# The stationary weights of the down blocks lie at 16 places within 256 bytes, 16 bytes apart, one place per block

## The chip, the core and the metric

The kernel runs on one core of a Trainium2 chip. The metric is the device time of one execution in microseconds. It was run three times, 2055.77, 2059.43 and 2058.96 us, so the median is 2058.96 us.

## What is computed

One transformer block on 256 tokens of width 2048, in float32: an attention and recurrence mixer, and then a layer that picks for every token and each of 8 heads 16 of 16384 experts. The part that matters here is that last layer. Every expert is one row of `down` and one row of `up`:

```python
def chunk(args):
    x_c, e_c, g_c = args
    act = jax.nn.gelu(jnp.einsum('td,thkd->thk', x_c, down[e_c]).astype(jnp.float32),
                      approximate=False) * g_c
    return jnp.einsum('thk,thkd->td', act.astype(up.dtype), up[e_c])
```

`e_c` are the experts picked and `g_c` their softmax weights. The picks come from a product of the token with `wq` (query), compared with keys.

## The kernel before

The kernel doesn't gather rows. It multiplies all 256 tokens by all 16384 rows of `down`, applies gelu, multiplies by a dense table of weights that is zero where an expert was not picked, and multiplies by all of `up`. The 16384 experts are cut into 32 down blocks (d0 to d31) of 512 experts. The 4 query blocks (wq0 to wq3) go through the same code.

A float32 product is made of three matmuls of rounded float32 values: every operand is split into a high part (`wh`, `xH`) and the rest (`wl`, `xL`), and hi*hi, hi*lo and lo*hi are added up in PSUM. `split` (lines 205 to 207) does it for a weight tile: ScalarE writes the high part, VectorE subtracts.

There are two ways to multiply.

- `mm_turn` (lines 365 to 374), for wq and the down blocks: a 128x128 piece of the weights is stationary, and the 256 tokens (`xH`, `xL`) stream by, 256 columns a matmul. One weight tile of 1024 columns makes 24 matmuls, and a block has 8 tiles, so 192 matmuls. Each of them has its own weight load (LDWEIGHTS).
- `mm_sub` (lines 359 to 363), for the mixer and the up blocks: the activations are stationary and the weights stream, 512 columns a matmul.

What sets the place of a weight tile is the list `items`, filled by `add_w` (lines 140 to 143) in the order in which the weights are used; its last field, `shift`, is the number of float32 elements by which the tile is pushed into a buffer that is 64 elements wider than the tile (`WROOM` is 1088). `next_part` (lines 282 to 314) takes the buffer, cuts the slice at `shift` (line 302) and splits into it. There are three buffers for the high and three for the low parts. `XTURN` (line 1049) pushes the streamed activations by 8 elements before the query blocks. `TURN`, 56, is the shift for all query and down blocks.

In the built program the weight buffers and the activations' buffers begin 32 bytes past a multiple of 256, and both the 1088 elements of a buffer (4352 bytes) and the steps between the 128-column pieces (512 bytes) are multiples of 256. "Place" below means the address modulo 256.

The order in time: the mixer up to some 470 us; then wq0 to wq3 and d0 to d13 (`LAG` is 14; lines 1275 to 1293), with the search of the picks and the table of weights (`w_build`, the lookup matmuls of line 1201) run beside them; from some 950 us the up blocks u, four to each of 16 groups, and between them d14 to d31, one down block in front of two up blocks (lines 1295 to 1322).

The gate matmuls of the mixer (`gate_logits`, `mm3`, lines 355 to 357) also have weights as the stationary operand: 16 slices of 24 columns that lie 96 bytes apart in one tile, three matmuls to a slice, with 256 tokens streaming by.

Of the kernel before, what the change touches and what calls it, by code (L numbers as in the profile page):

```python
# [47 lines left out]
TURN, WROOM, XTURN = 56, 1088, 8  # L48
# [19 lines left out]
def kernel(  # L68
# [71 lines left out]
    def add_w(src, n=4096, shift=0):  # L140
        for o in range(0, n, 2048):
            m = min(2048, n - o)
            items.append(("w", src[:, o:o + m], (m + 1023) // 1024, min(m, 1024), shift))
# [20 lines left out]
    nmix = len(items)  # L164
    for j in range(4):
        for h in range(2):
            add_w(wq[j, h], shift=TURN)
    for e in range(LAG):
        for h in range(2):
            add_w(down[e, h], shift=TURN)  # L170
    for g in range(NUG):
        for o in range(2):
            e = 2 * g + 2 + o
            if LAG <= e < NEB:
                for h in range(2):
                    add_w(down[e, h], shift=TURN)
            for q in range(2):
                add_w(up[g, 2 * o + q])
                if 4 <= g < 8:
                    items.append(("ada", 4 * (g - 4) + 2 * o + q))  # L180
# [1237 lines left out]
```

## Time and profile before

| | |
|---|---|
| median of three runs | 2058.96 us |
| the profiled execution | 2058.44 us, of which the span 2056.4 us |
| granted TensorE clock, mean | 0.986 |
| TensorE (PE) busy | 1984.4 us, 97% |
| weight loads (PEld) busy | 1758.6 us, 86% |
| VectorE (DVE) busy | 1451.1 us, 71% |
| ScalarE (ACT) busy | 1017.4 us, 49% |

PE are matmuls and PEld their weight loads, which overlap with them. Matmuls overlap with each other too: one of 256 columns has a duration of about 280 ns, but the next one starts after 113 to 118 ns. The step from one start to the next is therefore read from starts and counts and not from durations. A group in the profile names the line, the engine, the operation, what it writes and reads (buffer numbers left out), the shapes and how often it ran.

### The profile page before, as it was taken

The page shows a single profiled execution, that of the slowest core. Times are in us where ns is not written, and L with a number is a line of the kernel's source. Part 1 is how long each engine was busy: PE and PEld are TensorE (multiplying, and loading weights), DVE is VectorE, ACT ScalarE, POOL GpSimd, SP SyncE. Part 2 cuts the span into 40 slices and gives each one's busy share as a digit, 9 for nine tenths or more (in the row PEclk, how much of TensorE's full clock was granted, in tenths as well). Part 3 has the DMA queues.
Part 4 walks back from the last instruction along what each step waited for, and adds up shares of the span by engine and source line. Part 5 has one row for each costly group of instructions (what it writes and reads, how often), then busy time and mean ns, then how long its engine had stood idle before and what let it go on. Part 6 is the DMA issues. An engine that isn't in the chain of part 4 may idle for free.

```text
span 2056.4 us, 31264 instructions
## 1 busy us (share of the span) xinstructions
PE 1984.4 (97%) x12602; PEld 1758.6 (86%) x12602; DVE 1451.1 (71%) x2149; ACT 1017.4 (49%) x1454; POOL 61.1 (3%) x95
## 2 busy tenths in 40 slices
PE   5999997998999999999999999999999999999998
PEld 4777665788999999999788789889999889999897
DVE  7888999987999666546767766675555555555566
ACT  3545675545447878644444434444444444444442
POOL 0000000000000000001000000000000000000000
PEclk8999998999999999999999999999999999999999
DMA  9898788995555666778767777776565666566563
GB/s 370 334 360 334 267 324 324 348 347 182 177 177 183 241 220 246 257 247 308 256 232 249 282 266 254 255 269 203 198 204 196 212 207 206 204 201 209 198 225 131
DMA packets 75873, 509.12 MB, mean 248 GB/s; under 512 B 8528, under 2 KB 9040, under 8 KB 20176
## 3 DMA queue, kind: packets, MB, share of 16 engines
q1 hardware_dynamic: 63792, 450.50, 60.6%
q0 software_dynamic: 11936, 56.63, 8.2%
q8 instruction: 98, 1.61, 0.3%
q14 instruction: 47, 0.39, 0.1%
HBM read 478.78 MB, written 28.31 MB: 247 GB/s over the span
## 4 chain that ended last, share of the span: by engine, by line
PE 76%; DVE 11%; issue 8%; DMA 3%; ACT 1%; POOL 0%; SPq 0%; DVEq 0%; POOLq 0%; ACTq 0%
PE d L373 11%; PE d L372 11%; PE d L374 10%; PE u L356 8%; PE u L357 8%; PE u L355 8%; DVE wl L207 3%; PE w L1201 3%; DVE av L228 3%; PE wq L373 2%; PE wq L372 2%; PE wq L374 1%; PE y L355 1%; PE y L357 1%; PE y L356 1%
## 5 line engine op out<-in xcount | busy, mean ns | idle before, releaser
L207 DVE TENSOR_TENSOR wl<-raw,wh 128x1024 fp32r<-128x1024 f32 x649 | 789.2, 1221 | 467.0 <-ACT wh L206 464.2
L206 ACT CAST wh<-raw 128x1024 fp32r<-128x1024 f32 x649 | 680.0, 1051 | 813.9 <-PE u L357 374.7
L372 PE MATMUL d<-xH,wh 128*128 128x256 f32 x2048 | 573.2, 280 | 0.0
L373 PE MATMUL d<-xL,wh 128*128 128x256 f32 x2048 | 570.3, 278 | 0.0
L374 PE MATMUL d<-xH,wl 128*128 128x256 f32 x2048 | 569.6, 278 | 0.2 <-DVE wl L207 0.2
L356 PE MATMUL u<-wl,ah 128*128 128x512 f32 x1024 | 399.6, 390 | 3.6 <-DVE wl L207 3.6
L355 PE MATMUL u<-wh,ah 128*128 128x512 f32 x1024 | 398.9, 390 | 0.0
L357 PE MATMUL u<-wh,al 128*128 128x512 f32 x1024 | 398.5, 389 | 0.0
L372 PEld LDWEIGHTS d<-xH,wh 128*128 128x128 f32 x2048 | 385.0, 188 | 0.7
L373 PEld LDWEIGHTS d<-xL,wh 128*128 128x128 f32 x2048 | 384.8, 188 | 0.8
L374 PEld LDWEIGHTS d<-xH,wl 128*128 128x128 f32 x2048 | 384.0, 187 | 0.4 <-DVE wl L207 0.4
L356 PEld LDWEIGHTS u<-wl,ah 128*128 128x128 f32 x1024 | 192.2, 188 | 45.2 <-DVE wl L207 6.0
L357 PEld LDWEIGHTS u<-wh,al 128*128 128x128 f32 x1024 | 192.3, 188 | 40.1
L355 PEld LDWEIGHTS u<-wh,ah 128*128 128x128 f32 x1024 | 192.2, 188 | 39.7
L228 DVE SCALAR_TENSOR_TENSOR av<-av,cb 128x2048 f32<-128x2048 f32 x64 | 145.9, 2285 | 5.5 <-DMA av<-in_ada_w_dram 5.5
L1185 DVE TENSOR_TENSOR oh<-con,idT 128x1024 f32<-128x1024 f32 x64 | 78.0, 1224 | 62.0 <-PE w L1201 62.0
L1206 ACT ACTIVATE oh<-oh,gT 128x128 f32<-128x128 f32 x256 | 83.3, 396 | 25.6 <-DVE oh L1185 25.4
L372 PE MATMUL wq<-xH,wh 128*128 128x256 f32 x256 | 72.7, 285 | 2.5 <-ACT xH L206 2.5
L373 PE MATMUL wq<-xL,wh 128*128 128x256 f32 x256 | 72.6, 284 | 0.0
L374 PE MATMUL wq<-xH,wl 128*128 128x256 f32 x256 | 72.2, 282 | 0.0
L1262 DVE TENSOR_TENSOR acc<-acc,u 128x512 f32<-128x512 f32 x112 | 71.6, 680 | 0.0
L1201 PE MATMUL w<-oh 128*128 128x128 f32 x512 | 69.7, 276 | 0.0
(359 smaller groups left out, 2002.5 us busy)
## 6 DMA issues: line engine op xcount, KB each, us to landing
raw<-in_down_dram SPq DMA_DIRECT2D x128, 1024.0 KB, 5.2
raw<-in_up_dram SPq DMA_DIRECT2D x128, 1024.0 KB, 5.2
av<-in_ada_w_dram SPq DMA_DIRECT2D x64, 1024.0 KB, 7.2
raw<-in_w_a_dram SPq DMA_DIRECT2D x32, 1024.0 KB, 9.3
raw<-in_ada_p_dram SPq DMA_DIRECT2D x16, 1024.0 KB, 6.9
raw<-in_w_out_dram SPq DMA_DIRECT2D x16, 1024.0 KB, 7.9
raw<-in_wq_dram SPq DMA_DIRECT2D x16, 1024.0 KB, 5.2
wd<-stg POOLq DMA_DIRECT2D x8, 2048.0 KB, 7.9
```

What stands on the lines that cost most here:

```text
L206: A.copy(dst_h, src)
L207: V.tensor_tensor(dst_l, src, dst_h.bitcast(F32), OP.subtract)
L228: V.scalar_tensor_tensor(out=t, in0=t, scalar=1.0, in1=cb, op0=OP.mult, op1=OP.mult, accum_out=m)
L355: T.matmul(o, ah, bh, start=first, stop=False)
L356: T.matmul(o, ah, bl, start=False, stop=False)
L357: T.matmul(o, al, bh, start=False, stop=last)
L372: T.matmul(o, wh[:, kk, ws], bH[:, kc], start=f and i % 2 == 0, stop=False)
L373: T.matmul(o, wh[:, kk, ws], bL[:, kc], start=False, stop=False)
L374: T.matmul(o, wl[:, kk, ws], bH[:, kc], start=False, stop=e and i % 2 == 1)
L1185: V.tensor_tensor(oh, iota.unsqueeze(1).unsqueeze(1).to_broadcast([P, 4, 2, P]), idT[:, 4 * q:4 * q + 4].unsqueeze(3).to_broadcast([P, 4, ...
L1201: T.matmul(wps[p_][:, k * P:(k + 1) * P], oh[:, k, 1], oh[:, k, 0], start=True, stop=True)
L1206: A.activation(ohs[p_][:, k, 0], ohs[p_][:, k, 0], AF.Copy, scale=gT[:, t:t + 1])
```

## The change

Down block e gets the shift 4 * (e mod 16) elements, 16 bytes more for each block; wq2 and wq3 get 56 and 60 elements; wq0 and wq1 keep 56. Modulo 256 the stationary pieces then lie at 32 + 16 * (e mod 16) for block e, where all of them lay at 0 before. On every engine the instructions and their order are the same in both built programs; only the addresses of the weight tiles differ.

```diff
     for j in range(4):
         for h in range(2):
-            add_w(wq[j, h], shift=TURN)
+            add_w(wq[j, h], shift=TURN if j < 2 else 4 * (12 + j))
     for e in range(LAG):
         for h in range(2):
-            add_w(down[e, h], shift=TURN)
+            add_w(down[e, h], shift=4 * (e % 16))
     for g in range(NUG):
         for o in range(2):
             e = 2 * g + 2 + o
             if LAG <= e < NEB:
                 for h in range(2):
-                    add_w(down[e, h], shift=TURN)
+                    add_w(down[e, h], shift=4 * (e % 16))
```

## Rows read from the trace of the kernel before

**Rows 1.** The page: busy shares; granted clock in 40 slices; the chain by engine.

```profile
PE 1984.4 (97%) x12602; PEld 1758.6 (86%) x12602; DVE 1451.1 (71%) x2149; ACT 1017.4 (49%) x1454; POOL 61.1 (3%) x95
...
PEclk8999998999999999999999999999999999999999
...
PE 76%; DVE 11%; issue 8%; DMA 3%; ACT 1%; POOL 0%; SPq 0%; DVEq 0%; POOLq 0%; ACTq 0%
```

**Rows 2.** TensorE's waits, 470 to 2056 us: total us, times, longest.

```profile
PE u L356 <- DVE wl L207: 3.6, 4, 1.5
```

**Rows 3.** Busy us by engine (instructions), 640 to 840 us.

```profile
640.00:840.00 200.00, 199.97 (x1713) 199.36 (x1712) 139.00 (x121) 164.08 (x369) 7.47 (x14) 1.00 0.62 225
```

**Rows 4.** The page: line 372 in the down blocks.

```profile
L372 PE MATMUL d<-xH,wh 128*128 128x256 f32 x2048 | 573.2, 280 | 0.0
```

**Rows 5.** Line 372, 860 to 940 us: count, then first and last start.

```profile
L372 PE MATMUL d<-xH,wh 128*128 128x256 f32 x227 | 63.3, 279 | 0.0
...
860.04 0.28 PE L372 MATMUL d<-xH,wh 128*128 128x256 f32 x1
...
939.89 0.28 PE L372 MATMUL d<-xH,wh 128*128 128x256 f32 x1
```

**Rows 6.** The same, 1220 to 1240 us.

```profile
L372 PE MATMUL d<-xH,wh 128*128 128x256 f32 x60 | 16.6, 276 | 0.0
...
1219.79 0.28 PE L372 MATMUL d<-xH,wh 128*128 128x256 f32 x1
...
1239.85 0.28 PE L372 MATMUL d<-xH,wh 128*128 128x256 f32 x1
```

**Rows 7.** The same, 1483.5 to 1505 us.

```profile
L372 PE MATMUL d<-xH,wh 128*128 128x256 f32 x62 | 17.3, 279 | 0.0
...
1483.41 0.28 PE L372 MATMUL d<-xH,wh 128*128 128x256 f32 x1
...
1504.96 0.28 PE L372 MATMUL d<-xH,wh 128*128 128x256 f32 x1
```

**Rows 8.** TensorE in order of time from 840.5 us: start, duration.

```profile
840.72 1.16 PE L1201 MATMUL w<-oh 128*128 128x128 f32 x8
...
841.84 0.28 PE L373 MATMUL d<-xL,wh 128*128 128x256 f32 x1
...
842.97 0.28 PE L374 MATMUL d<-xH,wl 128*128 128x256 f32 x1
```

**Rows 9.** Line 355, 1000 to 1100 us: count, first and last start.

```profile
L355 PE MATMUL u<-wh,ah 128*128 128x512 f32 x148 | 57.6, 389 | 0.0
...
999.99 0.39 PE L355 MATMUL u<-wh,ah 128*128 128x512 f32 x1
...
1099.94 0.39 PE L355 MATMUL u<-wh,ah 128*128 128x512 f32 x1
```

**Rows 10.** The lookup matmuls, 16 in a row: start, duration of all.

```profile
703.10 1.95 PE L1201 MATMUL w<-oh 128*128 128x128 f32 x16
```

**Rows 11.** The gate matmuls in order of time (four starts of 45).

```profile
262.14 0.28 PE L355 MATMUL gl<-xH,wh 128*24 128x256 f32 x1
...
265.49 0.28 PE L357 MATMUL gl<-xH,wl 128*24 128x256 f32 x1
...
266.51 0.28 PE L357 MATMUL gl<-xH,wl 128*24 128x256 f32 x1
...
267.21 0.28 PE L357 MATMUL gl<-xH,wl 128*24 128x256 f32 x1
```

**Rows 12.** Up matmuls behind a down block, in order of time.

```profile
1459.08 0.40 PE L356 MATMUL u<-wl,ah 128*128 128x512 f32 x1
1459.32 0.39 PE L357 MATMUL u<-wh,al 128*128 128x512 f32 x1
```

**Rows 13.** Line 206 (min/median/max ns): 865 to 940, then 1000 to 1100 us.

```profile
L206 ACT CAST wh<-raw x27: 1049/1049/1052, 865.1 to 938.6; 128x1024 fp32r<-128x1024 f32 x27
...
L206 ACT CAST wh<-raw x37: 1042/1055/1058, 1000.9 to 1098.8; 128x1024 fp32r<-128x1024 f32 x37
```

## Prediction

> **What bounds the kernel now.** I read the engines' busy shares first, then the waits of TensorE, then the two stretches of the program in which the down blocks run. TensorE is busy 97% of the span, and the chain that ended last lies on it for 76% [rows 1]. From 470 us on TensorE waits for hardly anything: its longest total there is 3.6 us for the low halves of the weights, in 4 places [rows 2]. While the lookup weights are built beside the down blocks (640 to 840 us) it is busy 199.97 of 200 us, against 139 us on VectorE and 164 us on ScalarE [rows 3]. So what a down block costs is the step from one matmul to the next, times the matmuls. Line 372 runs 2048 times in the 32 down blocks, 64 times in each [rows 4]; with lines 373 and 374 that is 192 matmuls a block, and a query block has the same code.
>
> The duration of one matmul in such a group (280 ns) is no step, since they overlap. The step comes from two starts and a count. Between 860 and 940 us, blocks d10 to d13, line 372 has 227 instructions, the first at 860.04 and the last at 939.89 us: 79.85 us for 226 rounds of three lines, 117.8 ns a matmul [rows 5]. Between 1220 and 1240 us, block d14, it has 60, from 1219.79 to 1239.85 us: 20.06 us for 59 rounds, 113.3 ns [rows 6]. The two stretches run the same three lines at the same shapes and with the granted clock in the tenth of full speed that the page writes as 9 throughout [rows 1], the 2.4 GHz level, with the stationary tile at the same place in 256 bytes and the moving tile at the same place too. One late block, d20, is at the early step: 62 instructions, 21.55 us for 61 rounds, 117.8 ns [rows 7]. And in the early stretch there is a short piece at the late step: behind the lookup matmuls at 840.72 us the starts run from 841.84 to 842.97 us, ten steps of 113 ns [rows 8]. So at one place there are two steps, 4.44 ns apart, each of which holds for hundreds of matmuls, and what decides is how the stream was entered.
>
> **What the two steps are.** An up matmul streams 512 columns and steps at 226.6 ns (148 of line 355 from 999.99 to 1099.94 us, 99.95 us for 147 rounds of three) [rows 9], which is twice 113.3. So 113.3 ns is the stream's own pace for 256 columns, and I take it as the floor: no place can bring a down block under it. The weight load has a pace of its own: the lookup matmuls of 128 columns, each with a load of 128, take 1.95 us for 16, and less the last one's duration, some 0.28 us as elsewhere, that is 1.67 us for 15 steps, 111 to 112 ns [rows 10]. In a down block the load is thus some 2 ns short of being the bound, and a longer delay of it shows. My reading is that the slow step is stream and load reading the same memory in an unlucky phase. That a place has a say in this is shown by the gate matmuls. There the stationary slice moves by 96 bytes every three matmuls, and the moving tile stays. From 262.14 to 267.21 us there are 44 steps, 115.2 ns on average, not quite half way from the fast step to the slow one; nine of them from 265.49 to 266.51 us are at 113.3 ns, and as the slice comes to the next two places the six from 266.51 to 267.21 us are at 116.7 ns [rows 11]. A change of 256 columns to 512 and of places also shows in the first up matmuls behind a down block: one starts at 1459.08 and the next at 1459.32 us, 240 ns where 226.6 is the steady step [rows 12].
>
> The Trainium skill, page "TensorE: Matmul & The Clock Gate", section "Step-by-step: what each phase is for", gives TensorE two independent read ports into this memory, one for the stream and one for the weights, with the next load running beside the current matmul. By that rule a place can do nothing to the step, and the sum would be zero; the two steps at one place disagree with it as far as they go, and it stands below as a rival. The Trainium skill's page "SBUF — State Buffer", section "Door 1: The DMA port swizzle", speaks of lines of 16 bytes; all sixteen places begin such a line, so by that too the sum would be zero, and no run here shows it yet.
>
> **The change part by part.** No instruction is added, removed or put elsewhere on any engine; only addresses differ. In the built program a stationary tile begins 32 bytes past a multiple of 256, so the shift of 56 elements (224 bytes) put every query and down block at place 0; the moving tiles are at 64. Afterwards wq0 to wq2 stay at 0, wq3 is at 16, and down block e at 32 + 16 * (e mod 16), modulo 256. Blocks d14 and d30 fall on 0 again.
> - Early blocks: wq3 and d0 to d13, 15 blocks, are at 117.8 ns and get a new place. One block is worth 192 * 4.44 ns = 0.85 us. If all took the floor, -12.8 us.
> - Late blocks: of d14 to d31, 16 get a new place; 15 of them are at the floor, and d20 isn't. If all 15 left the floor for 117.8 ns, +12.8 us; d20 can give back 0.85 us.
> - A step above 117.8 ns: the highest the trace shows is 240 ns for 512 columns, 120 ns for 256 [rows 12]. All changed blocks there would be 15 * 192 * 6.7 ns = +19.3 us late and 16 * 192 * 2.2 ns = +6.8 us early and in d20, +26 us: the upper bound. The lower is -13.7 us.
> - The writers of the weights: ScalarE takes 1049 ns at the median for a tile written to place 0 and 1055 ns to place 32 [rows 13]. So few ns are covered: at 860 to 940 us a pair of tiles lasts 24 * 117.8 ns = 2.83 us, and TensorE waits 3.6 us for VectorE's part in all (rows 2). I cost it at nothing, a gain or a loss; without cover 6 ns on the 248 pairs of 31 moved blocks would be 1.5 us.
> - A gain in the early blocks counts in full: in rows 3 neither VectorE nor ScalarE is near the span.
>
> Between the bounds I take shares. For the stream's side I take half the places as slow (the mean of rows 11 is nearest to that). There a stationary slice has 24 columns and its load has time to spare; in a down block the load is nearly the bound, and if it is hit as often on its own, a place is good with 1/2 * 1/2 = 1/4 and slow with 3/4. Late: 3/4 * 12.8 = +9.6 us. Early: 1/4 * 12.8 = -3.2 us. d20: 1/4 * 0.85 = -0.2 us. Sum +6.2 us. The profiled execution took 2058.44 us (a span of 2056.4), the median of three runs is 2058.96 us, half a microsecond more; 2058.44 + 6.2 = 2064.6 us.
>
> **The rivals.**
> - Forecast, the late stretch loses more than the early one wins: 2064.6 us; by slow shares from two thirds to all, 2062 to 2071 us. For it: the late blocks can only lose. Against it: they are entered from up blocks that run at the stream's own pace (rows 9), and may keep it at any place. Chance 0.43.
> - The early blocks win and the late ones hold (the other side): the floor is found at three places of four early, -9.6 us, one late block in four slips, +3.2 us, d20 gives 0.6 us: -7.0 us, 2051.4 us. It decides as soon as the share of early blocks at the floor is over that of late ones off it by a third (4.1 of 12.8 us). For it: the piece in rows 8 shows that the early stretch is close to the floor even at place 0. Against it: the same entry, 16 short matmuls that step at the load's pace, comes again and again in that stretch, and 678 steps of rows 5 are slow without a break. Chance 0.20.
> - Halves: the average of rows 11 holds everywhere, the late loss and the early gain are 6.4 us each, d20 -0.4 us: 2058.0 us. Chance 0.18.
> - The place does nothing and history alone decides, so that the change does not do what moving a place is to do: 0 us, 2058.4 us. For it: one place has both steps. Against it: rows 11. The two rules cited above would give this. Chance 0.14.
> - A third, worse step at 120 ns nearly everywhere: 2084 us. Rows show it for single matmuls alone, never held. Chance 0.05.
>
> **How the numbers follow.** 0.2% of the time is 4.1 us, about what runs of this kernel can tell from none. Slower: most of the forecast's 0.43 (its low end is within the bound), the last rival, a bit of the halves: 0.44. Faster: the second case and a bit of the halves: 0.22. Within: 0.34. The range leaves out the last rival, the far end of the second and the tail of the forecast: 2051 to 2072 us; the forecast's own is 2062 to 2071 us.
>
> **What would show it.** Starts and counts of line 372, block by block. The forecast is right if most late blocks step at 117 ns or more while most early ones still do; d14 and d30, whose place is unchanged, and wq0 to wq2 are the controls. If blocks 16 apart (d0 and d16, d13 and d29) have the same step, the place decides; if early and late differ at one place, the entry does. Steps under 113.3 ns would show my floor wrong, steps of 120 ns or more held over a block the upper bound. Idle time of TensorE for VectorE much over 3.6 us would show the writers uncovered. The prediction is wrong if early blocks go to the floor in larger number than late ones leave it.

## The result: slower, by more than the range allowed

The changed kernel took 2075.29 us (median of 2075.08, 2075.29 and 2077.33) against 2058.96 us before: a ratio of 1.0087, with an interval from 1.0064 to 1.0110. That is 16 us slower. The forecast was 2064.6 us and the range ended at 2072.

The page of the changed kernel has the same numbers of instructions and the same clock as [rows 1], and its group of line 372 answers to [rows 4]. The chain that ended last still lies on TensorE for most of its length, though its share falls from 76 to 72%.

```profile
PE 1997.8 (96%) x12602; PEld 1772.8 (86%) x12602; DVE 1450.8 (70%) x2149; ACT 1017.4 (49%) x1454; POOL 61.0 (3%) x95
...
PEclk8999998999999999999999999999999999999999
...
PE 72%; DVE 12%; issue 9%; DMA 5%; ACT 2%; POOL 1%; SPq 0%; DVEq 0%; POOLq 0%; ACTq 0%
...
L372 PE MATMUL d<-xH,wh 128*128 128x256 f32 x2048 | 578.8, 283 | 0.0
```

TensorE's longest wait from 470 us on (total us, times, longest) answers to [rows 2]: it grew by 1.1 us. The writers of the weights stayed covered.

```profile
PE u L356 <- DVE wl L207: 4.7, 4, 1.7
```

The down blocks' steps again come from first and last starts of line 372, 64 instructions and so 63 rounds of three a block. The rows are d12 (place 224), d14 (0), d18 (64) and d22 (128) of the changed kernel: start, duration of one.

```profile
909.60 0.29 PE L372 MATMUL d<-xH,wh 128*128 128x256 f32 x1
...
932.28 0.29 PE L372 MATMUL d<-xH,wh 128*128 128x256 f32 x1
...
1223.14 0.28 PE L372 MATMUL d<-xH,wh 128*128 128x256 f32 x1
...
1244.56 0.28 PE L372 MATMUL d<-xH,wh 128*128 128x256 f32 x1
...
1399.96 0.28 PE L372 MATMUL d<-xH,wh 128*128 128x256 f32 x1
...
1422.62 0.28 PE L372 MATMUL d<-xH,wh 128*128 128x256 f32 x1
...
1580.24 0.28 PE L372 MATMUL d<-xH,wh 128*128 128x256 f32 x1
...
1601.70 0.28 PE L372 MATMUL d<-xH,wh 128*128 128x256 f32 x1
```

d12 takes 22.68 us for 189 steps, 120.0 ns; in [rows 5] it was 117.8. d14, which kept place 0, is at 113.3 ns as in [rows 6]. d18 is at 22.66 us / 189 = 119.9 ns and d22 at 21.46 / 189 = 113.5 ns. Done for all blocks (mean of the steps between neighbours of a block, those over 135 ns left out as breaks), with the distance written as place of the stationary piece less place of the stream, modulo 256:

| distance | place | early blocks, ns | late blocks, ns |
|---|---|---|---|
| 0 | 64 | d2 119.9 | d18 119.9 |
| 16 | 80 | d3 118.3 | d19 118.4 |
| 32 | 96 | d4 118.5 | d20 118.3 |
| 48 | 112 | d5 117.8 | d21 117.8 |
| 64 | 128 | d6 114.4 | d22 113.5 |
| 80 | 144 | d7 118.8 | d23 118.7 |
| 96 | 160 | d8 117.5 | d24 117.4 |
| 112 | 176 | d9 120.1 | d25 120.0 |
| 128 | 192 | d10 118.7 | d26 118.7 |
| 144 | 208 | d11 120.0 | d27 116.7 |
| 160 | 224 | d12 120.0 | d28 120.0 |
| 176 | 240 | d13 118.1 | d29 118.1 |
| 192 | 0 | wq0 to wq2 117.8 | d14, d30 113.3 |
| 208 | 16 | wq3 116.7 | d15, d31 116.7 |
| 224 | 32 | d0 117.8 | d16 116.7 |
| 240 | 48 | d1 119.1 | d17 119.9 |

Blocks at one place agree within 0.2 ns in eleven of the sixteen rows, though they stand hundreds of us apart and have other work around them. Two of the early means are mixtures: behind a break in the stream d1 goes from 117.3 to 120.0 ns, and d6 from 117.8 to some 114 ns. Times 192 matmuls, and less the steps before, the late blocks lose 13.3 us and the early ones 1.8 us. The profiled executions differ by 2075.08 - 2058.44 = 16.6 us; of the 1.5 us left, 1.1 us lie ahead of the first query block (it starts at 474.02 us, 472.91 before), where nothing was changed.

### The profile page after: what moved, and what is told of

Its sections match the earlier page's. It is cut to its first block, busy times and chain, and to the rows that moved or that the text cites. A ratio compares the mean times of both kernels' runs of the same rounds, so it can differ in the third digit from the quotient of the medians.

```text
span 2073.2 us, 31264 instructions
## 1 busy us (share of the span) xinstructions
PE 1997.8 (96%) x12602; PEld 1772.8 (86%) x12602; DVE 1450.8 (70%) x2149; ACT 1017.4 (49%) x1454; POOL 61.0 (3%) x95
## 4 chain that ended last, share of the span: by engine, by line
PE 72%; DVE 12%; issue 9%; DMA 5%; ACT 2%; POOL 1%; SPq 0%; DVEq 0%; POOLq 0%; ACTq 0%
PE d L374 11%; PE d L372 11%; PE d L373 11%; PE u L356 7%; PE u L357 7%; PE u L355 7%; DVE wl L207 3%; PE w L1201 3%; DVE av L228 3%; DMA raw<-in_ada_w_dram 2%; PE y L357 1%; PE y L355 1%; PE y L356 1%; DMA av<-in_ada_w_dram 1%; PE wq L372 1%
## 5 line engine op out<-in xcount | busy, mean ns | idle before, releaser
L207 DVE TENSOR_TENSOR wl<-raw,wh 128x1024 fp32r<-128x1024 f32 x649 | 788.9, 1220 | 477.8 <-ACT wh L206 477.3
L372 PE MATMUL wq<-xH,wh 128*128 128x256 f32 x256 | 73.1, 286 | 2.5 <-ACT xH L206 2.5
```

The costliest lines, as they stand in the source:

```text
L207: V.tensor_tensor(dst_l, src, dst_h.bitcast(F32), OP.subtract)
L372: T.matmul(o, wh[:, kk, ws], bH[:, kc], start=f and i % 2 == 0, stop=False)
```

## The experiments

Five theories came first. A: the step depends on the distance between the stationary piece and the stream. B: it depends on the stationary place alone. C: not the place, but its change from block to block disturbs the stream. And of how it acts: D, a bad place delays the weight load, or E, it delays the stream. E1 to E4 ran on one chip beside the kernel before (median 2062.93 us there), E5 to E8 on another (2061.93 us). E2, E3, E4 and E7 ran once each and are read by the steps in their traces.

### E1: all blocks at place 128

```diff
-TURN, WROOM, XTURN = 56, 1088, 8
+TURN, WROOM, XTURN = 24, 1088, 8
```
(on the kernel before)

> All query and down blocks at place 128 (the shift is 24 elements everywhere). Theory A, the place counts by its distance from the streamed tile at 64, and theory B, it counts by itself, both expect what d6 and d22 showed in the changed kernel: early blocks at 113.3 to 114.4 ns a matmul instead of 117.8, late ones at 113.3 to 113.5, d20 too. That is 18 * 192 * 3.4 to 4.4 ns + 0.8 us = 12 to 16 us less than before: 2043 to 2047 us. Theory C, not the place but the change of place from block to block disturbs the stream: the same as before, 2059 us, early 117.8 and late 113.3 ns.

Measured: 2051.55 us, a ratio of 0.9953 to the kernel before, interval 0.9937 to 0.9968: faster, by some 10 us, where A and B had 12 to 16. The rows are d10 and d14, start and duration of one:

```profile
859.52 0.28 PE L372 MATMUL d<-xH,wh 128*128 128x256 f32 x1
...
880.94 0.28 PE L372 MATMUL d<-xH,wh 128*128 128x256 f32 x1
...
1213.41 0.28 PE L372 MATMUL d<-xH,wh 128*128 128x256 f32 x1
...
1234.87 0.28 PE L372 MATMUL d<-xH,wh 128*128 128x256 f32 x1
```

d10 steps at 21.42 us / 189 = 113.3 ns where the early blocks had 117.8, d14 at 21.46 / 189 = 113.5 ns. C is out: with one place for all blocks the time is neither that of the kernel before nor that of the changed one. Not every block is at the fast step: d2 is at 117.8 ns and d3 at 116.4, which come behind waits for the picks, and d20 at 117.8, behind the transposes, as it was before. Its count between 1478 and 1499 us, and the first and last start of it:

```profile
L372 PE MATMUL d<-xH,wh 128*128 128x256 f32 x60 | 16.9, 281 | 0.0
```

```profile
1477.87 0.28 PE L372 MATMUL d<-xH,wh 128*128 128x256 f32 x1
...
1498.72 0.28 PE L372 MATMUL d<-xH,wh 128*128 128x256 f32 x1
```

20.85 us for 59 rounds, 117.8 ns. So distance 64 has the slow step too, but is thrown into it more seldom. By the blocks' steps the gain is 12.7 us early less 0.6 us late, some 12 us; the middle of the interval is 9.7 us, and the 12 lie within it. A part did not arrive: in the two profiled executions the time from the first query matmul to the end of the span is 8.5 us shorter. From the first matmul of d0 to that of d3 it took 73.1 us before and 73.6 us now, although d0 and d1 step faster, which is 2 us of the gap; in that stretch TensorE's waits for VectorE (the picks, and the low halves of the weights) grew by 1.2 us. Another 1.2 us are missing in d4 to d9, among the lookup matmuls; why isn't shown.

### E2: all blocks at place 64

```diff
-TURN, WROOM, XTURN = 56, 1088, 8
+TURN, WROOM, XTURN = 8, 1088, 8
```
(on the kernel before)

> All query and down blocks at place 64 (shift of 8 elements everywhere), the place of the stream itself. Theories A and B: 119.8 ns in early and late blocks alike, as d2 and d18 of the changed kernel: 19 * 192 * 2.1 ns + 17 * 192 * 6.6 ns = 29 us more than before, 2088 us. Theory C: 2059 us, with 117.8 and 113.3 ns.

Measured: 2088.74 us. d18, first and last start:

```profile
1407.91 0.28 PE L372 MATMUL d<-xH,wh 128*128 128x256 f32 x1
...
1430.57 0.28 PE L372 MATMUL d<-xH,wh 128*128 128x256 f32 x1
```

22.66 us / 189 = 119.9 ns, and 119.5 to 120.0 ns in all 36 blocks. As A and B had it; C is out a second time.

### E3: the sixteen places with the stream at 128

```diff
-TURN, WROOM, XTURN = 56, 1088, 8
+TURN, WROOM, XTURN = 56, 1088, 24
```
(on the changed kernel)

> The changed kernel with its sixteen places, but the streamed tiles moved from place 64 to 128. Theory A (distance): the pattern over the places moves by 64: late blocks at 64 and 192 (d18, d26) go to 113.5 ns, the one at 128 (d22) to 119.9, the one at 0 (d30) to 118.7; early d2 and d10 are the best of the early ones. Theory B (the stationary place alone): as in the changed kernel, 0 and 128 at 113.3 to 113.5 ns, 64 at 119.9, 192 at 118.7. The total tells little: about 2075 us by both.

Measured: 2073.88 us. First and last starts of d18 (place 64), d22 (128) and d26 (192):

```profile
1397.76 0.28 PE L372 MATMUL d<-xH,wh 128*128 128x256 f32 x1
...
1420.02 0.28 PE L372 MATMUL d<-xH,wh 128*128 128x256 f32 x1
...
1577.43 0.28 PE L372 MATMUL d<-xH,wh 128*128 128x256 f32 x1
...
1600.10 0.28 PE L372 MATMUL d<-xH,wh 128*128 128x256 f32 x1
...
1755.65 0.28 PE L372 MATMUL d<-xH,wh 128*128 128x256 f32 x1
...
1777.07 0.28 PE L372 MATMUL d<-xH,wh 128*128 128x256 f32 x1
```

d22 fell from the fast step to 22.67 us / 189 = 119.9 ns, and d26 rose to it: 21.42 / 189 = 113.3 ns, at place 192, which was at 118.7 ns with the stream at 64. So the distance counts, A, and B is out. Set against the table above by distance, the late blocks of the two kernels agree within 0.2 ns in fourteen of sixteen rows. The two others are 144 (116.7 there, 120.0 here) and 192 (113.3 there, and 22.26 us / 189 = 117.8 ns for d18 here), the same 192 that had both steps in the kernel before. The tiles' addresses are those of the changed kernel, so what writes the weights has no part in it. The expectation had d18 fast, and the early d2, also at distance 192, among the best (117.8 ns); it missed that 192 has two steps.

### E4: the up blocks' stationary activations at sixteen places

```diff
-        h = pool.tile([P, 4, S], F32R, tag="ah", bufs=4, name=f"ah{eb}")
-        l = pool.tile([P, 4, S], F32R, tag="al", bufs=4, name=f"al{eb}")
+        h, l = [pool.tile([P, 4 * S + 64], F32R, tag=f"a{n}", bufs=4, name=f"a{n}{eb}")[:, 4 * (eb % 16):4 * (eb % 16) + 4 * S]
+                .rearrange("p (c t) -> p c t", t=S) for n in "hl"]
```
(on the kernel before)

> The kernel before (down blocks at place 0), with the stationary activations of the up blocks at 32 + 16 * (e mod 16) instead of 32, their stream of 512 columns at 32 as before. Theory D, a bad place delays the weight load, which is the bound only where the stream is as short as the load: with 512 columns the load has over 110 ns to spare, all up blocks stay at 226.6 ns a matmul, 2059 us within 3. Theory E, a bad place delays the stream itself: the up blocks take up to 13 ns more a matmul, on the mean of the places 5 to 9 ns on 3072 matmuls, 15 to 28 us more, 2074 to 2087 us.

Measured: 2082.28 us. The page's group of line 355 has a longer mean (390 ns before):

```profile
L355 PE MATMUL u<-wh,ah 128*128 128x512 f32 x1024 | 403.1, 394 | 0.0
```

Line 355 within one half of an up block, first and last of 8 instructions, at place 48 and then at place 144 (the stream is at 32):

```profile
1441.41 0.39 PE L355 MATMUL u<-wh,ah 128*128 128x512 f32 x1
...
1446.17 0.39 PE L355 MATMUL u<-wh,ah 128*128 128x512 f32 x1
...
1710.04 0.40 PE L355 MATMUL u<-wh,ah 128*128 128x512 f32 x1
...
1714.95 0.39 PE L355 MATMUL u<-wh,ah 128*128 128x512 f32 x1
```

4.76 us for 7 rounds of three, 226.7 ns, at distance 16; 4.91 us, 233.8 ns, at distance 112. Over all of them: 227 to 228 ns at the distances 240, 0 and 16, 229.4 to 230.2 at 176 and 192, and 231.6 to 234.4 elsewhere. A weight load that has over 110 ns to spare (226.7 less the 111 to 112 of [rows 10]) can't be what shows here, so the stream itself is delayed: E. Its size was not E's: at most 7.7 ns a matmul, where E had up to 13, against 6.7 ns at half the columns. So the delay goes by the matmul and not by the columns that stream; each matmul has one load, but what holds the stream up isn't shown. The up blocks account for some 14 us of the 24 us that the span grew, below E's 15 to 28, and that the total fell into E's range is luck. The other 10 us are in the down blocks, of which nothing was changed: 13 of the 18 late ones are now at the slow step, 12 more than before. d16:

```profile
1314.68 0.28 PE L372 MATMUL d<-xH,wh 128*128 128x256 f32 x1
...
1336.94 0.28 PE L372 MATMUL d<-xH,wh 128*128 128x256 f32 x1
```

22.26 us / 189 = 117.8 ns at place 0, where it had 113.3. With its own addresses as they were, only what ran ahead of it differs, so at distance 192 the entry decides, as the prediction had read from [rows 7, 8]. By what rule isn't clear: d17 to d19, behind up halves at the distances 240 and 16 that keep 226.7 ns, stay fast, and the blocks behind the slow halves at 48, 112, 144, 176 and 208 are slow; but d23 and d24, behind a half at distance 80 and 231.7 ns, stay fast too.

### E5 and E6: one half of the change at a time

```diff
 E5, on the changed kernel: late blocks alone
-            add_w(wq[j, h], shift=TURN if j < 2 else 4 * (12 + j))
+            add_w(wq[j, h], shift=TURN)
     for e in range(LAG):
         for h in range(2):
-            add_w(down[e, h], shift=4 * (e % 16))
+            add_w(down[e, h], shift=TURN)
 E6, on the changed kernel: early blocks alone
             if LAG <= e < NEB:
                 for h in range(2):
-                    add_w(down[e, h], shift=4 * (e % 16))
+                    add_w(down[e, h], shift=TURN)
```

> The change in d14 to d31 alone; wq0 to wq3 and d0 to d13 stay at place 0. By the steps measured in the changed kernel the late blocks lose 13.5 us (the sum over them of 192 * (step - step before)), so 13 to 14 us more than before, a ratio of 1.0065. Had the early blocks been what cost (theory C in its early form), within 3 us of before.

> The change in wq2, wq3 and d0 to d13 alone; d14 to d31 stay at place 0. By the steps measured in the changed kernel the early blocks lose 1 to 2 us on balance (d6 wins 0.7 us, d2, d9, d11 and d12 lose 0.4 to 0.5 us each): a ratio of 1.000 to 1.001. By the terms of the prediction, which gave the early blocks a gain of 3.2 us: a ratio of 0.998.

Measured: E5 2077.15 us, ratio 1.0063 (1.0045 to 1.0082), 13 us. E6 2062.51 us, ratio 1.0005 (0.9994 to 1.0016), 1 us. The late blocks are nearly the whole loss, and the early blocks gave nothing back; the 0.998 that the prediction's gain of 3.2 us would be lies outside E6's interval. One early block of E6 differs from the changed kernel: d11 (distance 144), with the same addresses and the same blocks in front of it. Its first and last start:

```profile
887.30 0.28 PE L372 MATMUL d<-xH,wh 128*128 128x256 f32 x1
...
909.67 0.28 PE L372 MATMUL d<-xH,wh 128*128 128x256 f32 x1
```

22.37 us / 189 = 118.4 ns, where it had 120.0. So at such a distance the step can differ from one execution to the next.

### E7: places 4 bytes apart around the good one

```diff
-TURN, WROOM, XTURN = 56, 1088, 8
+TURN, WROOM, XTURN = 24, 1088, 8
-            add_w(wq[j, h], shift=TURN if j < 2 else 4 * (12 + j))
+            add_w(wq[j, h], shift=TURN)
-            add_w(down[e, h], shift=4 * (e % 16))
+            add_w(down[e, h], shift=16 + e % 16)
```
(on the changed kernel; the last line in both places)

> Sixteen places 4 bytes apart, 96 to 156, one per block, around the good place 128 (stream at 64); the query blocks at 128. Theory F1, the place counts in units of 16 bytes: the late blocks at 128 to 140 (d24 to d27) are all at 113.5 ns, those at 112 to 124 (d20 to d23) all at 117.8, those at 144 to 156 (d28 to d31) at 118.7. Theory F2, every 4 bytes count: only d24 is at 113.5, with d23 and d25 between it and the neighbours 16 bytes off, 114 to 118.

Measured: 2076.5 us. First and last starts of d21 (place 116), d23 (124), d24 (128) and d25 (132):

```profile
1536.49 0.28 PE L372 MATMUL d<-xH,wh 128*128 128x256 f32 x1
...
1557.94 0.28 PE L372 MATMUL d<-xH,wh 128*128 128x256 f32 x1
...
1624.52 0.28 PE L372 MATMUL d<-xH,wh 128*128 128x256 f32 x1
...
1647.10 0.28 PE L372 MATMUL d<-xH,wh 128*128 128x256 f32 x1
...
1669.24 0.28 PE L372 MATMUL d<-xH,wh 128*128 128x256 f32 x1
...
1690.69 0.28 PE L372 MATMUL d<-xH,wh 128*128 128x256 f32 x1
...
1712.86 0.28 PE L372 MATMUL d<-xH,wh 128*128 128x256 f32 x1
...
1735.21 0.28 PE L372 MATMUL d<-xH,wh 128*128 128x256 f32 x1
```

113.5, 119.5, 113.5 and 118.3 ns. Every 4 bytes count, so F1 is out; but F2's slope is missing as well: beside 128 the step is at once among the slow ones, and 116 and 152 (d30, 113.4 ns) are as fast. At 140 the early block d11 has 113.4 ns and the late one, d27, 120.0. Four places 12 bytes apart, then, with at least one of them of two steps. Here wq0, at place 128 and entered from a wait, is at 117.8 ns and wq2 and wq3 at 113.5. Why 12 bytes, no run says.

### E8: the good distance at other places

```diff
-TURN, WROOM, XTURN = 56, 1088, 8
+TURN, WROOM, XTURN = 40, 1088, 24
```
(on the kernel before)

> All query and down blocks at place 192 with the stream at 128: the distance of the faster version (64 bytes), both places moved. Theory A (distance): 113.3 to 114 ns in all blocks but those entered from a wait, the same time as with 128 and 64, 0.9953 of before within 0.0015. Theory B (the place alone): 118.7 ns everywhere as at 192 in the changed kernel, 18 * 192 * 0.9 + 17 * 192 * 5.4 ns = 21 us more than before, 1.010.

Measured: 2052.06 us, ratio 0.9951 (0.9934 to 0.9968), as E1. d14:

```profile
1207.43 0.28 PE L372 MATMUL d<-xH,wh 128*128 128x256 f32 x1
...
1228.85 0.28 PE L372 MATMUL d<-xH,wh 128*128 128x256 f32 x1
```

21.42 us / 189 = 113.3 ns, as in all late blocks but d20. With both places moved and the distance kept the time is kept: A.

## Why the prediction was wrong

- **TensorE's step from matmul to matmul as the cost, with 113.3 ns as its floor.** Right. No block of any of the nine new kernels stepped below 113.3 ns, and the blocks' steps times 192 give 15.1 of the 16.6 us.
- **The late blocks can only lose, the early ones hold either way.** Right in its bounds: E5 puts 13 us on the late blocks, where the bound for them was +19.3 us, and the whole, 16 us, lies between -13.7 and +26 us.
- **The shares, where it failed.** A place was taken as good with 1/4, in both stretches alike, because the gate matmuls were at the slow step about half the time and the load was to be hit as often again. Of the 15 new places one is good. E4 takes the ground from the second half: at 512 columns the delay shows with the load far from being the bound. The matmuls of [rows 10], from which the load was taken to be nearly the bound in a down block, are of plain float32, and the trace has two records for each of them (512 for 256 in the kernel): their 111 ns bound the load's pace from above, and whether they are the load's or the stream's isn't shown. And the gate matmuls have stationary slices of 24 columns where a down block has 128; a share taken from them was no share of these. For the early blocks this made a gain of 3.2 us, where 1.8 us were lost: a term of the wrong sign, and E6 rules it out. For the late ones 14 of 15 at 117.8 ns would be 11.9 us where 9.6 stood.
- **One slow step of 117.8 ns.** Mis-sized. It is the slow step of the distances 192 and 48. Others have their own, from 116.7 to 120.0 ns; the mean over d15 to d29, one for each new place, is 118.0 with the fast one in it. That takes the late loss from 11.9 to 13.3 us. In the early blocks it makes the sign: d6 alone won 0.7 us, and the other 14, which the prediction had at 117.8 ns or better, went to 118.7 on the mean and lost 2.5 us. The 120 ns were in the prediction as a rival that holds nearly everywhere; they hold at four or five places of sixteen.
- **The entry.** Right that it decides at place 0 (E4, d16), and the likely reason why the early blocks had the slow step there. In the changed kernel blocks of one distance differ by 0.8 ns or more at 64, 144, 192, 224 and 240; at the other eleven the distance alone gives the step. The prediction took the phase for the thing and the place for a draw; at most distances it is the other way round.
- **An early gain counts in full.** Not quite: E1's early blocks gained what their steps say in wq0 to wq3 and d10 to d13, but only 3.1 of 4.3 us in d4 to d9, and nothing between d0 and d3, where TensorE's waits for VectorE grew as its steps fell. The prediction had looked at the busy shares of 640 to 840 us only [rows 3].
- **The writers.** Right for this change: 4.7 us of waits against 3.6, and E3 keeps the writers' addresses and moves the pattern.
- **The rival that the place does nothing.** The Trainium skill, page "TensorE: Matmul & The Clock Gate", section "Step-by-step: what each phase is for", has the stream and the weights on two independent read ports. The prediction drew from it a sum of zero. The runs disagree: the step depends on where the two operands lie to each other (E3, E8), however many ports there are.

## What to carry to other kernels

Where float32 operands rounded for TensorE stream past loads of 128 columns, as here, the distance of the two operands' addresses modulo 256 is a parameter like a tile size, worth up to 6% of each matmul: 113.3 to 120.0 ns at 256 columns, and 226.7 to 234 at 512, where other distances are the good ones (0 and 16 either way). Much of it can be read in one run that gives each block its own place, by the step from start to start; durations in the groups (276 to 283 ns) hide it. A place that is fast in one stretch can be slow in another, so look for one that is fast behind most kinds of entry. Here that was 64 bytes, which was still slow in d20 and d2 (E1) and in wq0 of E7, and made the kernel 0.5% faster than before.

## What was not expected of the hardware

- A stream of 256 columns at the 2.4 GHz level never went below 113.3 ns a matmul, and one of 512 not below 226.6 on the mean of a steady stretch: the same floor per column, and no place went under it.
- At most distances the step is reproduced within 0.2 ns between blocks, kernels and chips, but at some it has two or three values, each held until the stream is broken: 113.3 and 117.8 ns at 192, 113.5 and 117.8 at 64, 116.7, 118.3 and 120.0 at 144. In a block with waits it can change at a wait: d1 of E1 goes from 117.8 to 113.3 ns.
- 4 bytes make the difference: 119.5, 113.5 and 118.3 ns at the distances 60, 64 and 68, and 113.4 to 113.5 ns at 52 and 88 too; 76 had 113.4 in one block and 120.0 in another.
